# State updates of the decoding streams: a masked stationary operand of 128 rows in place of 32 of its rows

## The chip, the cores and the metric

The kernel runs on one core of a Trainium2 chip. The metric is the device time of one execution in microseconds. TensorE multiplies a stationary operand (up to 128 rows by 128 columns, loaded by an instruction of its own) with a moving operand of the same rows. VectorE, ScalarE and GpSimd work on the 128 partitions of the on-chip memory SBUF, SP issues DMAs.

## The reference

One step of a two-layer streaming encoder: 512 new frames of one prompt, and 16 new frames of each of 8 running streams. Layer 0 is a feed-forward block, then a mixer of four mLSTM heads and sixteen Mamba-2 (SSD) heads, then a feed-forward block; layer 1 has the same with eight gated-DeltaNet heads as its mixer. Each head of each stream carries a state matrix, and the update of these states is what the change touches:

```
C = decay * C + einsum('brh,brhd,brhe->bhde', wr, k, v)                       # mLSTM, 128 x 256 per stream and head
S = exp(bL) * S + einsum('brgj,brgjp,brgn->bgjpn', exp(bL - b) * dt, x, bm)   # SSD, 64 x 128
S = exp(gL) * S + einsum('bhr,bhrd,bhre->bhde', exp(gL - gam), kh, u)         # DeltaNet, 128 x 128
```

The sum over r runs over the 16 frames of one stream. All states of the streams are outputs.

## The kernel before, in words

All 640 frames stand side by side: 512 of the prompt (four tiles of 128) and 8 x 16 = 128 of the streams (tile 4). Matrices of the weights are split into a high and a low part (`split`, ScalarE and GpSimd), and each projection is made of three passes over the parts (`mmT` L225, `projR` L770, `wout` L733; L427 and L494 in the feed-forward blocks). These split operands take one pass of TensorE each; plain fp32 operands, which the recurrences use, take two.

In the mixers the projections are the main line. The recurrences are generators in a list; after six or twelve passes of a projection `tick` advances every generator to its next `yield`. So a step of a recurrence is traced between two packets of projections, and the framework then orders each engine's instructions by the order of tracing and by what is free. `side_by_side` advances a head's prompt and its streams in turn. `until` ticks on without projections where the main line needs a result.

In tile 4 stream b holds the partitions 16 b to 16 b + 15. A row slice starts at a multiple of 32, so one product takes the 32 rows of a pair of streams (g = b // 2), and one of the two operands is zeroed for the other stream of the pair by `par`, a [128, 2] constant with the parity of each partition's stream.

- mLSTM (`mlstm_head`, inner generator `streams`): `kw[:, 4 + e]` holds the weighted keys of tile 4 with parity e alone, made from PSUM at L1289. For each b of 8 one product `kw[32g : 32g + 32, 4 + e]` (stationary) with `v[32g : 32g + 32, 4]` (L1341), then a `yield`, then the update of `Cb[b]` on VectorE (L1343) and its DMA out.
- SSD (`ssd_quad`, inner generator `running(i)`, i = 0, 1): after transposes (L1524) and products of 32 columns (L1531) for each half, two products of 32 rows, `xw[r, 4, ...]` with `Bz[r]` (L1538), where `Bz` holds both parities (L1415).
- DeltaNet (`gdn_streams`, one per head): at the end of a head's chain ScalarE writes `wz`, both parities of w (L2044); then for each g of 4 one product `kw[r, tok]` with `wz[r]` (L2050), two updates on VectorE (L2054) and a DMA per half.

`tmp()` gives one of three rotating SBUF buffers of 128 x 668. A convolution (`conv`, L930 to L963) takes two of them, `gdn_sumsq` one (L1762), `sumsq` and some others one. PSUM in the mixers: two pairs of banks ("big") for projections, four single banks ("small") for the recurrences. ScalarE and VectorE work strictly in order.

Of the kernel before, what the change touches and what calls it, by code (L numbers as in the profile page):

```python
# [11 lines left out]
AF = mybir.ActivationFunctionType  # L12
ALU = mybir.AluOpType
# [3 lines left out]
P = 128  # L17
# [14 lines left out]
class Raw:  # L32


    def __init__(self, load, n=0):
        self.fetch, self.n, self.then, self.v = load, n, None, None
# [17 lines left out]
class Trunk:  # L54
    def __init__(self, ctx, tc, io):
        self.tc, self.nc, self.io = tc, tc.nc, io
        self.cst = ctx.enter_context(tc.tile_pool(name="cst", bufs=1))
        self.sb = ctx.enter_context(tc.tile_pool(name="sb", bufs=1))
        self.dram = ctx.enter_context(tc.tile_pool(name="dram", bufs=2, space=bass.MemoryType.DRAM))
        self.n = 0  # L60
        self.pending = []
        self.bg = []
        self.early = {}
        self.rows = None
        self.ahead = 0
        nc = self.nc

        self.ident = self.const([P, P], "ident")
        make_identity(nc, self.ident)
        self.ones = self.const([P, 1], "ones")  # L70
        nc.vector.memset(self.ones, 1.0)

        self.zero = self.const([P, 1], "zero")
        nc.vector.memset(self.zero, 0.0)


        self.U, self.Ub, self.Bk = (self.const([P, P], n) for n in ("U", "Ub", "Bk"))
        for m in (self.U, self.Bk):
            nc.gpsimd.memset(m, 1.0)
        nc.gpsimd.affine_select(  # L80
            out=self.U, in_=self.U, pattern=[[1, P]], compare_op=ALU.is_ge, fill=0.0, base=0, channel_multiplier=-1
        )
        bk = self.Bk.rearrange("p (b s) -> p b s", s=16)
        nc.gpsimd.affine_select(
            out=bk, in_=bk, pattern=[[-16, 8], [0, 16]], compare_op=ALU.is_ge, fill=0.0, base=0, channel_multiplier=1
        )
        nc.gpsimd.affine_select(
            out=bk, in_=bk, pattern=[[16, 8], [0, 16]], compare_op=ALU.is_ge, fill=0.0, base=15, channel_multiplier=-1
        )
        nc.vector.tensor_tensor(self.Ub, self.U, self.Bk, ALU.mult)  # L90

        self.par = self.const([P, 2], "par")
        st = self.Bk.rearrange("p (g e s) -> p e g s", e=2, s=16)
        for e in range(2):
            nc.vector.tensor_reduce(self.par[:, e : e + 1], st[:, e, :, 0], axis=AX, op=ALU.add)

        self.x = [self.const([P, T], f"x{d}") for d in range(ND)]
        self.xg = [None] * ND
        self.xs = [None] * (ND // 2)
# [1171 lines left out]
    def mlstm_head(self, ab, tile, h, qT, kT, v, sig, qz, nO, nP):  # L1271
        nc, io = self.nc, self.io
        Cb = []
        for b in range(8):
            c = tile("Cb", [P, 257], bufs=8)
# [9 lines left out]
        kw = tile("kw", [P, 6, P], bufs=1)  # L1285
# [39 lines left out]
        def streams():  # L1325
            qs = qT[:, 512:].rearrange("p (g e s) -> p g e s", e=2, s=16)
            qd = qz.rearrange("p (g e) s -> p g e s", e=2)
            for e in range(2):
                nc.scalar.copy(qd[:, :, e, 16 * e : 16 * e + 16], qs[:, :, e])
            yield  # L1330
            inter = self.small()
            for e in range(2):
                for g in range(4):
                    b = 2 * g + e
                    nc.tensor.matmul(inter[32 * g : 32 * g + 32, :257], lhsT=qz[:, b], rhs=Cb[b], start=(e == 0), stop=(e == 1))
            yield
            yield from numerator(4, inter)
            for b in range(8):
                g, e = b // 2, b % 2
                st = self.small()  # L1340
                nc.tensor.matmul(st[:, :257], lhsT=kw[32 * g : 32 * g + 32, 4 + e], rhs=v[32 * g : 32 * g + 32, 4], start=True, stop=True)  # L1341
                yield
                nc.vector.scalar_tensor_tensor(Cb[b], Cb[b], self.dec[:, h, 4 + b : 5 + b], st[:, :257], ALU.mult, ALU.add)  # L1343
                nc.sync.dma_start(out=io["s_C"][b, h], in_=Cb[b][:, :256])
                nc.scalar.copy(nO[:, b * 4 + h : b * 4 + h + 1], Cb[b][:, 256:257])

        yield from self.side_by_side(prompt(), streams())

        den = num[:, :, 256]
# [12 lines left out]
        for e in range(2):  # L1362
# [5 lines left out]
            i = 56 + 2 * h + e  # L1368
# [96 lines left out]
    def ssd_quad(self, tile, u, x, B, Bz, CT, cz, CB):  # L1465

        nc, io = self.nc, self.io
# [16 lines left out]
        xw = tile("xw", [P, NT, 256])  # L1484
# [30 lines left out]

        def running(i):

            inter = self.small()
            j = 2 * u + i
            for hf in range(2):  # L1520
                s0 = S0[2 * i + hf]
                ps = self.small()
                for b in range(4):
                    nc.tensor.transpose(ps[:, b * P : (b + 1) * P], s0[:, b], self.ident)  # L1524
                yield
                S0T = tile("S0T", [P, 4, P], bufs=1)
                nc.scalar.copy(S0T.rearrange("p a b -> p (a b)"), ps)
                for e in range(2):
                    for gg in (2 * hf, 2 * hf + 1):
                        bb = 2 * gg + e  # L1530
                        nc.tensor.matmul(  # L1531
                            inter[32 * gg : 32 * gg + 32, :P], lhsT=cz[:, bb], rhs=S0T[:, bb - 4 * hf], start=(e == 0), stop=(e == 1)
                        )
                yield
                for gg in (2 * hf, 2 * hf + 1):
                    r = slice(32 * gg, 32 * gg + 32)
                    st = self.small()
                    nc.tensor.matmul(  # L1538
                        st[:, :256], lhsT=xw[r, 4, i * P : (i + 1) * P], rhs=Bz[r].rearrange("p a b -> p (a b)"), start=True, stop=True
                    )  # L1540
                    yield
                    for e in range(2):
                        b = 2 * gg + e
                        o = s0[:, b - 4 * hf]
                        nc.vector.scalar_tensor_tensor(o, o, self.dS[:, j, b : b + 1], st[:, e * P : (e + 1) * P], ALU.mult, ALU.add)
                nc.sync.dma_start(out=io["s_ssd"][4 * hf : 4 * hf + 4, 2 * j : 2 * j + 2].rearrange("b h p n -> (h p) b n"), in_=s0)
            y1 = tile("y1", [P, 2, 256])[:, 0, :P].rearrange("p (h d) -> p h d", h=2)
            h = h0 + 2 * i
            nc.vector.tensor_tensor(
                y1,  # L1550
                inter[:, :P].rearrange("p (h d) -> p h d", h=2),
                self.eb[:, 4, h : h + 2].rearrange("p (h o) -> p h o", o=1).to_broadcast([P, 2, 64]),
                ALU.mult,
            )
            o = x[:, 4, i * P : (i + 1) * P]
            nc.vector.tensor_tensor(o, o, y1.rearrange("p h d -> p (h d)"), ALU.add)
# [440 lines left out]
    def gdn_streams(self, tile, h, x, qT, kT, kws, QKs, hl, kqz, square):  # L1997

        nc, io = self.nc, self.io
        t, tok = 4, slice(512, T)  # L2000
# [12 lines left out]
        for g2 in range(2):  # L2013
            ps = self.small()
            for e in range(2):
                for gl in range(2):
                    g = 2 * g2 + gl
# [3 lines left out]
            for gl in range(2):  # L2021
                g = 2 * g2 + gl
# [5 lines left out]
        V, kw, QK = self.Us[h], kws[hl], QKs[hl]  # L2028
        nc.vector.scalar_tensor_tensor(x, kq[:, 0], self.neg[:, h, t : t + 1], x, ALU.mult, ALU.add)
        yield  # L2030
        ps = self.small()
# [5 lines left out]
        ps = self.small()  # L2037
# [4 lines left out]
        wz = kq  # L2042
        for e in (1, 0):
            nc.scalar.activation(out=wz[:, e], in_=w, func=AF.Copy, scale=self.par[:, e : e + 1])  # L2044
        yield
        for g in range(4):
            r = slice(32 * g, 32 * g + 32)
            s0 = S0[g // 2]
            ps = self.small()
            nc.tensor.matmul(ps[:, :256], lhsT=kw[r, tok], rhs=wz[r].rearrange("p a b -> p (a b)"), start=True, stop=True)  # L2050
            for e in range(2):
                b = 2 * g + e
                j = b % 4
                nc.vector.scalar_tensor_tensor(s0[:, j], s0[:, j], self.egs[:, b, h : h + 1], ps[:, e * P : (e + 1) * P], ALU.mult, ALU.add)  # L2054
            if g % 2:
                nc.sync.dma_start(out=io["s_gdn"][4 * (g // 2) : 4 * (g // 2) + 4, h].rearrange("b d e -> d b e"), in_=s0)
            yield

    def gdn_z(self, tile, i):

        zs = tile("zs", [P, NT, 256])
        for t, ps in self.projR(self.w_in, 3072 + 256 * i):
            self.nc.scalar.activation(out=zs[:, t], in_=ps, func=AF.Tanh, scale=self.rch[:, t : t + 1])
            self.nc.vector.scalar_tensor_tensor(zs[:, t], zs[:, t], 1.0, ps, ALU.add, ALU.mult)  # L2064
        self.zs[i] = zs
# [139 lines left out]
```

## Time and profile before

| | |
|---|---|
| median of 3 runs | 2993.99 us (2993.27 to 2996.22) |
| the profiled execution's own time | 2991.16 us |
| its span, first to last instruction | 2989.4 us |
| mean granted TensorE clock | 0.979 of 2.4 GHz |
| TensorE matmuls busy | 2889.4 us |
| TensorE weight loads busy | 2777.9 us |
| VectorE, ScalarE, GpSimd busy | 1877.5, 1250.4, 1478.5 us |

"PE" in the rows is TensorE's matmuls, "PEld" its weight loads, "DVE" VectorE, "ACT" ScalarE, "POOL" GpSimd, "SPq" the queue of SP. A row of the order of time merges neighbouring instructions of one kind: "x2" at a matmul of fp32 operands is one product in two passes. The end of a matmul is modelled, so starts are what to compare.

### The profile page before, as it was taken

The numbers are of one execution on the slowest core, as the hardware profiler recorded it, in microseconds if no ns is written. First come the engines' busy times: TensorE is split into PE (matmuls) and PEld (weight loads), VectorE is DVE, ScalarE is ACT, GpSimd is POOL, SyncE is SP. The second block draws the span as 40 slices with busy tenths as digits, with TensorE's granted clock in tenths as the row PEclk, the third lists the DMA queues.
The fourth block names the chain that finished last, engine by engine and source line by source line (L and its number), as shares of the span: only waits on it lengthen the run. The fifth ranks groups of instructions, "written<-read, shape, count | busy, mean of one in ns | idle before, by whom it ended". The sixth has DMA issues, their size and how long they took to land. (4 is left out here: it accounts for less than half of the span.)

```text
span 2989.4 us, 51425 instructions
## 1 busy us (share of the span) xinstructions
PE 2889.4 (97%) x19910; PEld 2777.9 (93%) x19910; DVE 1877.5 (63%) x3547; ACT 1250.4 (42%) x2655; POOL 1478.5 (49%) x1039
## 2 busy tenths in 40 slices
PE   8999999999999999999999999999999999999997
PEld 7999998988989889999998999999888898999996
DVE  7756655233566677766657666666777756865664
ACT  5333334333344344333344333334555454433334
POOL 3767662222223126776646767633323232677663
PEclk9999999999999999999999999999999999999999
DMA  3322222222213221322221322221221212222212
GB/s 104 106 75 82 76 80 59 87 87 87 84 56 90 73 79 58 102 82 76 81 87 60 99 74 83 75 78 50 64 68 47 85 54 84 71 85 85 85 64 85
DMA packets 243112, 232.14 MB, mean 78 GB/s; under 512 B 22135, under 2 KB 219908, under 8 KB 242870
## 3 DMA queue, kind: packets, MB, share of 16 engines
q1 hardware_dynamic: 242870, 228.87, 25.0%
q8 instruction: 158, 2.59, 0.4%
q14 instruction: 84, 0.69, 0.1%
HBM read 210.23 MB, written 18.60 MB: 77 GB/s over the span
## 5 line engine op out<-in xcount | busy, mean ns | idle before, releaser
L617 POOL TENSOR_TENSOR wsp<-wraw,wsp 128x512 fp32r<-128x512 f32 x600 | 892.2, 1500 | 556.3 <-ACT wsp L616 546.1
L208 POOL TENSOR_TENSOR wsp<-wraw,wsp 128x512 fp32r<-128x512 f32 x216 | 293.4, 1366 | 829.6 <-ACT wsp L207 517.5
L494 PE MATMUL small<-h,wsp 128*128 128x320 f32 x4032 | 597.9, 309 | 0.0
L427 PE MATMUL small<-xg,wsp 128*128 128x320 f32 x3840 | 588.2, 310 | 10.0 <-ACT wsp L616 6.2
L494 PEld LDWEIGHTS small<-h,wsp 128*128 128x128 f32 x4032 | 593.1, 188 | 0.0
L427 PEld LDWEIGHTS small<-xg,wsp 128*128 128x128 f32 x3840 | 570.9, 189 | 12.2 <-ACT wsp L616 7.3
L616 ACT ACTIVATE wsp<-wraw 128x512 fp32r<-128x512 f32 x600 | 364.3, 626 | 373.6 <-PE small L427 216.0
L225 PE MATMUL big<-xg,wsp 128*128 128x320 f32 x2112 | 368.7, 323 | 0.0
L225 PEld LDWEIGHTS big<-xg,wsp 128*128 128x128 f32 x2112 | 321.9, 193 | 21.6 <-issue 20.5
L617 POOL TENSOR_TENSOR wsp<-S,wsp 128x512 fp32r<-128x512 f32 x160 | 250.5, 1577 | 72.0 <-ACT wsp L616 45.0
L427 PE MATMUL small<-extA,wsp 128*128 128x320 f32 x1440 | 254.6, 312 | 1.0 <-POOL wsp L617 1.0
L770 PE MATMUL big<-wsp,xg 128*128 128x256 f32 x1920 | 244.3, 284 | 1.5 <-DVE zs L2064 1.4
L770 PEld LDWEIGHTS big<-wsp,xg 128*128 128x128 f32 x1920 | 233.2, 188 | 4.2 <-DVE zs L2064 2.1
L207 ACT ACTIVATE wsp<-wraw 128x512 fp32r<-128x512 f32 x216 | 136.2, 633 | 224.7 <-PE big L225 99.8
L427 PEld LDWEIGHTS small<-extA,wsp 128*128 128x128 f32 x1440 | 224.2, 190 | 2.5 <-POOL wsp L617 2.3
L454 DVE TENSOR_TENSOR up<-small,up 128x320 f32<-128x320 f32 x200 | 97.5, 488 | 201.3 <-PE small L427 201.2
L454 DVE TENSOR_TENSOR gate<-small,gate 128x320 f32<-128x320 f32 x200 | 97.9, 490 | 143.9 <-PE small L427 142.5
L427 PE MATMUL small<-extB,wsp 128*128 128x320 f32 x960 | 180.9, 310 | 0.0
L579 DVE SCALAR_TENSOR_TENSOR x<-small,x 128x320 f32<-128x320 f32 x368 | 157.9, 480 | 29.9 <-PE small L494 29.1
L485 ACT ACTIVATE h<-up 128x1280 fp32r<-128x1280 f32 x40 | 51.0, 1274 | 263.8 <-DVE up L483 263.8
L427 PEld LDWEIGHTS small<-extB,wsp 128*128 128x128 f32 x960 | 152.0, 189 | 0.0
L616 ACT ACTIVATE wsp<-S 128x512 fp32r<-128x512 f32 x160 | 99.3, 627 | 112.2 <-PE small L427 59.6
(469 smaller groups left out, 4057.6 us busy)
## 6 DMA issues: line engine op xcount, KB each, us to landing
wraw<-in_ffn_w_up SPq DMA_DIRECT2D x43, 1024.0 KB
wraw<-in_ffn_w_gate SPq DMA_DIRECT2D x43, 1024.0 KB
wraw<-in_ffn_w_down SPq DMA_DIRECT2D x38, 1024.0 KB
wraw<-in_ab_w_in SPq DMA_DIRECT2D x16, 1024.0 KB
wraw<-in_gdn_w_in SPq DMA_DIRECT2D x16, 1024.0 KB
wraw<-in_ffn_w_down SPq DMA_DIRECT2D x16, 512.0 KB
wraw<-in_ab_w_out SPq DMA_DIRECT2D x32, 256.0 KB
wraw<-in_ab_w_in SPq DMA_DIRECT2D x12, 512.0 KB
```

The lines of the kernel that those rows point to most:

```text
L207: nc.scalar.activation(out=hi, in_=src[:, i : i + n], func=AF.Copy)
L208: nc.gpsimd.tensor_tensor(lo, src[:, i : i + n], hi.bitcast(F32), ALU.subtract)
L225: self.nc.tensor.matmul(ps[:, half, :HT], lhsT=wp, rhs=ap[:, half * HT : half * HT + HT], start=(k == 0 and i == 0), stop=(k == n - 1 and ...
L427: self.nc.tensor.matmul(ps, lhsT=unit.parts[wp][:, k], rhs=acts[k][:, ap], start=(first and k == 0 and i == 0), stop=(last and k == ND // ...
L454: nc.vector.tensor_tensor(c(dst), bank[b], c(src), ALU.add)
L485: nc.scalar.activation(out=hi, in_=u, func=AF.Copy)
L494: self.nc.tensor.matmul(out[half], lhsT=wp, rhs=ap[:, half * HT : half * HT + HT], start=(first and i == 0), stop=(last and i == 2))
L579: nc.vector.scalar_tensor_tensor(x[:, i], out[i], 0.5, x[:, i], ALU.mult, ALU.add)
L616: nc.scalar.activation(out=u.parts[0], in_=src, func=AF.Copy)
L617: nc.gpsimd.tensor_tensor(u.parts[1], src, u.parts[0].bitcast(F32), ALU.subtract)
L770: self.nc.tensor.matmul(ps[:, t % 2, :256], lhsT=ap[:, t * P : (t + 1) * P], rhs=wp, start=(k == 0 and i == 0), stop=(k == ND - 1 and i == 2))
```

## The change

Two constants are added beside `par`: `one` [128, 8], whose column b is one at the partitions of stream b and zero elsewhere, and `duo` [128, 4], the same for the pairs of streams. A stationary operand is then copied by ScalarE with such a column as its scale per partition, so that the rows of the other streams are zero, and the product runs over all 128 rows.

- mLSTM: before streams 0 and 4 of a head, four copies (one per stream) into a "tmp" buffer, then a `yield`; the products use all rows of `kb` and `v`.
- SSD: a new helper `per_duo` makes four copies (one per pair) into a "tmp" buffer at the start of `running(i)`.
- DeltaNet: `per_duo` of the keys after `wz`, then a `yield`.

Four 128 x 128 copies make one group; there are 8 groups per mixer kind. The number of products, their outputs, updates and DMAs stay.

```diff
+        self.one = self.const([P, 8], "one")
+        nc.vector.tensor_copy(self.one, bk[:, :, 0])
+        self.duo = self.const([P, 4], "duo")
+        od = self.one.rearrange("p (g e) -> p g e", e=2)
+        nc.vector.tensor_tensor(self.duo, od[:, :, 0], od[:, :, 1], ALU.add)
...
             for b in range(8):
                 g, e = b // 2, b % 2
+                if b % 4 == 0:
+                    kb = self.tmp()[:, :512].rearrange("p (b c) -> p b c", b=4)
+                    for i in range(4):
+                        nc.scalar.activation(out=kb[:, i], in_=kw[:, 4 + i % 2], func=AF.Copy, scale=self.one[:, b + i : b + i + 1])
+                    yield
                 st = self.small()
-                nc.tensor.matmul(st[:, :257], lhsT=kw[32 * g : 32 * g + 32, 4 + e], rhs=v[32 * g : 32 * g + 32, 4], start=True, stop=True)
+                nc.tensor.matmul(st[:, :257], lhsT=kb[:, b % 4], rhs=v[:, 4], start=True, stop=True)
                 yield
...
         def running(i):
 
+            xg = self.per_duo(xw[:, 4, i * P : (i + 1) * P])
             inter = self.small()
...
-                    r = slice(32 * gg, 32 * gg + 32)
                     st = self.small()
                     nc.tensor.matmul(
-                        st[:, :256], lhsT=xw[r, 4, i * P : (i + 1) * P], rhs=Bz[r].rearrange("p a b -> p (a b)"), start=True, stop=True
+                        st[:, :256], lhsT=xg[:, gg], rhs=Bz.rearrange("p a b -> p (a b)"), start=True, stop=True
                     )
...
+        kg = self.per_duo(kw[:, tok])
+        yield
         for g in range(4):
-            r = slice(32 * g, 32 * g + 32)
             s0 = S0[g // 2]
             ps = self.small()
-            nc.tensor.matmul(ps[:, :256], lhsT=kw[r, tok], rhs=wz[r].rearrange("p a b -> p (a b)"), start=True, stop=True)
+            nc.tensor.matmul(ps[:, :256], lhsT=kg[:, g], rhs=wz.rearrange("p a b -> p (a b)"), start=True, stop=True)
...
+    def per_duo(self, src):
+
+        out = self.tmp()[:, :512].rearrange("p (g c) -> p g c", g=4)
+        for g in range(4):
+            self.nc.scalar.activation(out=out[:, g], in_=src, func=AF.Copy, scale=self.duo[:, g : g + 1])
+        return out
```

## Rows read from the trace of the kernel before

**Rows 1.** The page: busy time, share of the span and instructions of each engine.

```profile
PE 2889.4 (97%) x19910; PEld 2777.9 (93%) x19910; DVE 1877.5 (63%) x3547; ACT 1250.4 (42%) x2655; POOL 1478.5 (49%) x1039
```

**Rows 2.** Busy time by stretch: PE, PEld, DVE, ACT, POOL, then clock, DMA.

```profile
545.00:770.00 225.00, 217.48 (x1476) 192.31 (x1476) 79.33 (x204) 81.17 (x242) 54.81 (x43) 0.98 0.28 84
842.00:1060.00 218.00, 214.06 (x1485) 186.42 (x1484) 143.23 (x328) 91.57 (x240) 50.15 (x36) 1.00 0.26 75
2140.00:2470.00 330.00, 320.20 (x2383) 290.06 (x2382) 226.73 (x669) 172.70 (x530) 87.18 (x75) 0.94 0.23 64
```

**Rows 3.** TensorE in order of time, first mLSTM head: start us, us, line, form.

```profile
550.23 0.59 PE L1311 MATMUL small<-extC,extB 128*128 128x257 f32 x2
550.66 0.60 PE L1313 MATMUL small<-v,kw 128*128 128x257 f32 x2
551.18 0.70 PE L1341 MATMUL small<-v,kw 32*128 32x257 f32 x2
```

**Rows 4.** The weight loads there; in brackets the idle time before them.

```profile
550.45 0.41 PEld L1313 LDWEIGHTS small<-v,kw 128*128 128x128 f32 x2
551.18 0.29 PEld L1341 LDWEIGHTS small<-v,kw 32*128 32x128 f32 x2 [0.33 <-issue]
551.81 0.44 PEld L225 LDWEIGHTS big<-xg,wsp 128*128 128x128 f32 x3 [0.33 <-issue]
```

**Rows 5.** TensorE in order of time: packets around 560, 1055 and 2234 us.

```profile
559.75 0.69 PE L1341 MATMUL small<-v,kw 32*128 32x257 f32 x2
...
561.46 0.70 PE L1341 MATMUL small<-v,kw 32*128 32x257 f32 x2
...
1054.16 0.69 PE L1538 MATMUL small<-Bz,xw 32*128 32x256 f32 x2
...
1055.87 0.69 PE L1538 MATMUL small<-Bz,xw 32*128 32x256 f32 x2
...
2233.21 0.69 PE L2050 MATMUL small<-kq,kw 32*128 32x256 f32 x2
...
2234.91 0.69 PE L2050 MATMUL small<-kq,kw 32*128 32x256 f32 x2
```

**Rows 6.** The page's groups: projection passes of the feed-forward blocks, busy us, mean ns.

```profile
L494 PE MATMUL small<-h,wsp 128*128 128x320 f32 x4032 | 597.9, 309 | 0.0
```

**Rows 7.** The three lines with 32 rows: passes, ns min/median/max, first and last start.

```profile
L1341 PE MATMUL small<-v,kw x64: 375/427/480, 548.6 to 765.7; 32*128 32x257 f32 x64
...
L1538 PE MATMUL small<-Bz,xw x64: 374/426/478, 842.7 to 1056.2; 32*128 32x256 f32 x64
...
L2050 PE MATMUL small<-kq,kw x64: 374/478/791, 2141.4 to 2460.7; 32*128 32x256 f32 x64
```

**Rows 8.** ScalarE's copy with a parity column as scale: ns min/median/max.

```profile
L2044 ACT ACTIVATE kq<-kq,par x16: 384/398/404, 2140.6 to 2453.3; 128x128 f32<-128x128 f32 x16
```

**Rows 9.** What TensorE waited for, 2140 to 2470: us, times, longest.

```profile
PE small L1785 <- DVE kap L1779: 2.1, 1, 2.1
...
PE small L2050 <- ACT kq L2044: 0.7, 2, 0.6
```

**Rows 10.** VectorE in order of time: a convolution and the next one's first step.

```profile
774.89 0.49 DVE L937 TENSOR_TENSOR tmp<-big,R 128x320 f32<-128x320 f32 x1 [1.02 <-PE big L225]
...
780.55 1.02 DVE L959 SCALAR_TENSOR_TENSOR extA<-tmp,tmp 128x512 f32<-128x512 f32 x2 [0.89 <-ACT tmp L956]
781.93 0.49 DVE L937 TENSOR_TENSOR tmp<-big,R 128x320 f32<-128x320 f32 x1 [0.36 <-PE big L225]
```

**Rows 11.** Weight loads by line, 545 to 770: busy, mean ns, idle before.

```profile
L1341 PEld LDWEIGHTS small<-v,kw 32*128 32x128 f32 x64 | 9.4, 183 | 9.0 <-issue 5.7 <-ACT extA L1303 1.3 <-DVE nr L357 1.2
...
L1311 PEld LDWEIGHTS small<-extC,extB 128*128 128x128 f32 x24 | 4.0, 188 | 0.0
```

**Rows 12.** Busy time in two stretches of the pairs (columns as in rows 2).

```profile
2254.60:2264.80 10.20, 10.20 (x35) 8.34 (x34) 7.05 (x18) 2.73 (x6) 0.50 (x2) 0.50 0.66 186
2336.50:2350.10 13.60, 13.60 (x51) 11.40 (x52) 6.64 (x19) 2.03 (x6) 1.52 (x2) 0.50 0.77 233
```

## The prediction

> **What bounds the kernel now.** I read the shares of the five engines first: TensorE is busy for 97% of the span, VectorE for 63%, ScalarE for 42% [rows 1]. Then the same shares in the three stretches that the change touches (545 to 770 us: mLSTM heads; 842 to 1060: SSD quads; 2140 to 2470: DeltaNet pairs): TensorE 217 of 225, 214 of 218 and 320 of 330 us, and no other engine over 70% [rows 2]. So in each of them the projections of the main line keep TensorE fed, and the recurrences run in the gaps between packets of six projection matmuls. A busy TensorE is not one at its peak, though, and the same rows show it: its weight loads are busy for only 192 of 225, 186 of 218 and 290 of 330 us, where elsewhere they follow the matmuls closely. Some time inside those stretches is counted as busy in which nothing new is loaded.
>
> The order of time on TensorE shows where. An fp32 product is two passes, each with its load. Two neighbouring products of 128 rows and 257 columns start 0.43 us apart [rows 3], so a pass is 0.215 us. The product of 32 rows behind them starts 0.52 us after its predecessor [rows 3], and the load of the next projection 0.63 us after that. On the load side the 128-row loads run on without a hole, while the first 32-row load stands 0.33 us idle, and so does the first projection load after it [rows 4]. The profile names no engine that the load waits for ("issue"). I read this as TensorE letting the matmuls in flight end before the rows in use change from 128 to 32, and again on the way back.
>
> **The price of one such product.** I take a clean packet: six projection passes and one 32-row product, nothing else. It repeats every 1.71 us in an mLSTM head, every 1.71 in an SSD quad, every 1.70 in a DeltaNet pair [rows 5]. A projection pass of 320 columns is 597.9 / 4032 = 0.148 us by the largest group of such passes [rows 6]; six are 0.89. A 128-row product is 0.43. 1.71 - 0.89 - 0.43 = 0.39 us is lost per product, whatever the stage. (It shows as about 0.09 ahead, 0.2 within, 0.1 behind.)
>
> **The change part by part.**
>
> *Removed: the 32-row products.* Each of the three lines has 64 passes, which is 32 products [rows 7]; 96 in all. Each stands alone among 128-row work, so each pays its switch in and out. With 128 rows the operands differ from the neighbours' in nothing but values. The sum: 96 x 0.39 = -37.4 us, on TensorE, in stretches where TensorE sets the pace. The matmul count stays at 96 x 2 passes; rows that the mask zeroes cost nothing extra if a 128-row pass costs its 0.215 us, as the neighbours' do. The bounds: nothing (if a masked product keeps the cost) and -37.4. I take -37.4, since the row nearest to the new product, with the same 128 x 257 shape [rows 3], is a measured one.
>
> *A rule that speaks against it.* The 128-row load of L1313 begins at 550.45 while the matmuls of L1311, of the same rows, run until 550.82 [rows 3, 4]. The Trainium skill, "TensorE: Matmul & The Clock Gate", section "Part 3: Packing small matmuls — row/col tiling", says that a weight load overlaps matmuls in flight only where its row group differs. By that rule a full-height load would stand bare on every pass, and the change would gain nothing; by the row the load is hidden and the sum is -37.4. The trace disagrees with the rule here, and I go by the trace.
>
> *Added: 96 masking copies on ScalarE.* 24 groups of four 128 x 128 copies with a scale per row: 8 in the heads (before stream 0 and stream 4), 8 in the quads (one per half quad), 8 in the pairs (one per head). The same operation, SBUF to SBUF with a mask column as scale, takes 0.40 us in L2044 [rows 8]: 1.6 us per group, 38 us in all. ScalarE is busy for 81 of 225, 92 of 218 and 173 of 330 us [rows 2], so the work fits. What hides it: in heads and pairs the generator yields after the copies, so a packet of projections (0.89 us) and whatever else is due stands ahead of the first product, which needs the first copy alone; in the quads two yields, four transposes and four 32-column products come first. Queued behind the copies on ScalarE are the splits of the next weights and the copies out of PSUM; both run ahead of TensorE by some packets. If the cover is gone, a group costs up to 1.6 us, 24 x 1.6 = 38 us. Where it is thin already is seen: twice TensorE waits for the masking copy L2044 right before L2050, 0.7 us together [rows 9]. There the four new copies come right after L2044; I take +2 us, between 0 and 38, near the row.
>
> *Added: two yields per head of the mLSTM, one per head of the DeltaNet.* Each moves the remaining steps of a stream, with their output DMAs and the loads that SP has queued behind them, one packet later (1.3 to 1.7 us). The main line makes its next demand on these heads many packets later, so I take 0; a bare step would cost its packet.
>
> *Added: the waits.* The products now wait for ScalarE's copy; behind one on TensorE's queue stand the next projections. ScalarE waits for a free "tmp" buffer; this is a rival below. In the forecast it costs nothing: a convolution holds its two of three buffers from 774.89 to 781.57 us, and the next starts its multiplications at 781.93, when both are free again [rows 10]. A third one held by the masked copies is one that the convolutions can do without, by 0.36 us.
>
> *Added: two small VectorE operations at the start* (a copy of 8 columns, a sum of 4). They stand behind a mask product that waits for the same GpSimd operation, long before their first use: 0.
>
> *Late next.* Where TensorE comes sooner to a product that waits for VectorE's chains, part of what is saved turns into waiting. The largest such wait in the pairs is 2.1 us, in one place [rows 9]. I take +1 us.
>
> **The sum.** -37.4 + 2 + 1 = -34.4 us on the profiled execution of 2991.16 us (span 2989.4, 1.8 around it): 2956.8. The median of the three runs lies 2.8 us above that execution, so 2959.6 for a median; I say 2959.
>
> **Rivals.**
>
> 1. *Nothing comes of it:* a full-height product in this place loses as much as a 32-row one, since each of its two loads (188 ns for the loads of L1311 [rows 11]) stands bare. 2 x 0.19 = 0.38 against 0.39 saved: about 2993. Against: the same rows show idle time ahead of the loads of L1341 (9.0 us over 64) and none ahead of those of L1311. Chance 0.05. (The rule of the Trainium skill that is weighed above would make this case; the overlap in the trace is why it gets no more.)
>
> 2. *The copies stand in front of the products* in half of the groups, because ScalarE is in order and a weight split of 0.6 us or a convolution step of 0.9 gets in between: 12 x 1.6 = 19 us given back, 2959 + 17 = 2976. For it: the two waits for L2044. Against: ScalarE's idle share. Chance 0.14.
>
> 3. *Slower, by the "tmp" buffers.* The copies of quads and pairs (16 groups) hold one of the three over the four products, some 7 us or more. If a convolution then has to wait for its second buffer, or the copies for a convolution's (up to the 6.7 us from 774.89 to 781.57), ScalarE or VectorE stands, the two PSUM pairs of the projections stay full, and TensorE stops. It decides at 37.4 / 16 = 2.3 us per group; at half a convolution, 3.35 us, it is +54 - 37 = +17: 3011. For it: the DeltaNet's squares take a "tmp" as well. Against: the 0.36 us above, and two PSUM pairs that let TensorE go on. Chance 0.07.
>
> 4. *More than the sum, by the clock.* Two stretches around the products of the pairs, 10.2 and 13.6 us, ran at a granted clock of 0.50, the lower level of 1.2 GHz [rows 12]; ahead of both TensorE had short waits, and thin work. Without the holes they may stay at 2.4 GHz: half of 23.8 us is 11.9, so 2947. Against: other thin work stays. Chance 0.10.
>
> The forecast itself has 0.64.
>
> **How the numbers follow.** What a measurement here can tell from no change is about 0.2%, 6 us. Faster: forecast, rivals 2 and 4, 0.88. Same: rival 1, 0.05. Slower: rival 3, 0.07. The range goes from 2949, which takes in part of rival 4, to 2975, which takes in the milder half of rival 2; left out are some 0.2: rivals 1 and 3 (0.12), and the outer parts of 2 and 4.
>
> **What would show it.** In the changed profile the clean packet of six projections and one product should repeat every 1.32 us in place of 1.71, in all three stages; the two passes of a product should last 0.59 to 0.60 us together, like those of L1311 and L1313 [rows 3], in place of 0.69 to 0.70 [rows 5]; the idle time ahead of its loads and ahead of the projections behind it should be gone. TensorE's waits for the new copies should stay under 4 us in all. Wrong would be: packets that stay at 1.7 us (rival 1), a wait of TensorE for the copies in the first rows of its waits (rival 2), waits for "tmp" ahead of convolutions or copies and TensorE idle behind them (rival 3), other stretches of the lower clock (rival 4).

## The result, and the profile after

The changed kernel takes 2947.25 us (median of 4 runs, 2944.59 to 2951.37); the kernel before took 2995.1 in the same sitting (4 runs). The ratio is 0.9847, with an interval from 0.9834 to 0.9859. The forecast was 2959: right in sign, 12 us too slow, and 2 us below the lower end of its range (2949). The profiled execution went from 2991.16 to 2948.21 us, which is -42.95 where the prediction's sum on that execution was -34.4.

The first line of the page of the profile, to be set against [rows 1]: TensorE's matmuls are busy for 50 us less, its loads for 5.5 us less, and ScalarE for 24 us more.

```profile
PE 2839.5 (96%) x19910; PEld 2772.4 (94%) x19910; DVE 1894.1 (64%) x3549; ACT 1274.1 (43%) x2751; POOL 1477.3 (50%) x1039
```

TensorE in order of time after the change, to be set against [rows 3, 5] (start us, us, line, form):

```profile
550.04 0.59 PE L1317 MATMUL small<-extC,extB 128*128 128x257 f32 x2
550.47 0.60 PE L1319 MATMUL small<-v,kw 128*128 128x257 f32 x2
550.90 0.59 PE L1352 MATMUL small<-v,tmp 128*128 128x257 f32 x2
551.15 1.25 PE L231 MATMUL big<-xg,wsp 128*128 128x320 f32 x6
...
558.80 0.59 PE L1352 MATMUL small<-v,tmp 128*128 128x257 f32 x2
...
560.11 0.60 PE L1352 MATMUL small<-v,tmp 128*128 128x257 f32 x2
...
1030.14 0.59 PE L1549 MATMUL small<-Bz,tmp 128*128 128x256 f32 x2
...
1031.46 0.59 PE L1549 MATMUL small<-Bz,tmp 128*128 128x256 f32 x2
...
2209.24 0.60 PE L2062 MATMUL small<-kq,tmp 128*128 128x256 f32 x2
...
2210.56 0.59 PE L2062 MATMUL small<-kq,tmp 128*128 128x256 f32 x2
```

The state product now stands in line like any other: it starts 0.43 us after L1319, as L1319 does after L1317, and the projection follows 0.25 later (0.63 before). The clean packet repeats every 1.31, 1.32 and 1.32 us in the three stages, where it was 1.71, 1.71 and 1.70. On the load side there, no idle time is left (it would stand in brackets at the end of a line), against 0.33 us twice in [rows 4]:

```profile
550.25 0.41 PEld L1319 LDWEIGHTS small<-v,kw 128*128 128x128 f32 x2
550.69 0.40 PEld L1352 LDWEIGHTS small<-v,tmp 128*128 128x128 f32 x2
551.12 1.01 PEld L231 LDWEIGHTS big<-xg,wsp 128*128 128x128 f32 x6
```

The three lines again, answering to [rows 7] (passes, ns min/median/max, first and last start):

```profile
L1352 PE MATMUL small<-v,tmp x64: 377/380/382, 550.9 to 753.8; 128*128 128x257 f32 x64
...
L1549 PE MATMUL small<-Bz,tmp x64: 377/378/484, 835.1 to 1037.2; 128*128 128x256 f32 x64
...
L2062 PE MATMUL small<-kq,tmp x64: 377/380/484, 2123.5 to 2418.3; 128*128 128x256 f32 x64
```

From first to last start, the heads' products shrink from 217.1 to 202.9 us, the quads' from 213.5 to 202.1, the pairs' from 319.3 to 294.8. The first two are -14.2 and -11.4, against -12.5 foreseen for each (32 x 0.39); the third is -24.5, twice what was foreseen. Why, the clock shows. Below are the mixer stages whole, first of the kernel before, then after (bounds from the first product of a mixer's input projections to the first down projection behind it; columns as in [rows 2]):

```profile
465.80:1109.40 643.60, 622.66 (x4312) 561.08 (x4313) 333.71 (x770) 256.34 (x679) 165.93 (x121) 0.99 0.26 78
...
1996.80:2521.00 524.20, 497.95 (x3679) 459.37 (x3679) 355.51 (x994) 269.84 (x766) 151.53 (x129) 0.94 0.22 63
```

```profile
467.30:1090.30 623.00, 599.33 (x4313) 570.13 (x4313) 335.07 (x770) 272.24 (x744) 163.96 (x121) 0.98 0.27 81
...
1977.10:2477.10 500.00, 473.77 (x3678) 447.08 (x3679) 357.11 (x993) 276.73 (x796) 152.51 (x129) 0.97 0.23 66
...
2122.00:2427.40 305.40, 294.70 (x2381) 277.18 (x2381) 227.62 (x675) 178.08 (x555) 88.05 (x74) 0.99 0.24 69
...
2172.00:2178.80 6.80, 6.66 (x28) 5.55 (x29) 2.43 (x8) 4.16 (x13) 1.72 (x2) 0.50 0.13 42
```

The DeltaNet stage went from 524.2 to 500.0 us while its clock rose from 0.94 to 0.97. Half clock is 1.2 in place of 2.4 GHz; among the pairs' products one stretch of it is left, 6.8 us long. [rows 12] show two, of 10.2 and 13.6 us, but the clock records of the trace of before hold six between 2140 and 2470 us, 41 us in all. Half of the 34 us that went is 17 of the -24.5, which leaves some 7 for the products. So the profile after already says that two things happened. The feed-forward stages did not move (887.4 and 886.8 us for the middle one).

### The profile page after: what moved, and what is told of

The parts are those of the page before. It is cut to its first block, busy times and chain, and to the rows that moved or that the text cites. A ratio compares the mean times of both kernels' runs of the same rounds, so it can differ in the third digit from the quotient of the medians.

```text
span 2946.5 us, 51522 instructions
## 1 busy us (share of the span) xinstructions
PE 2839.5 (96%) x19910; PEld 2772.4 (94%) x19910; DVE 1894.1 (64%) x3549; ACT 1274.1 (43%) x2751; POOL 1477.3 (50%) x1039
## 5 line engine op out<-in xcount | busy, mean ns | idle before, releaser
L214 POOL TENSOR_TENSOR wsp<-wraw,wsp 128x512 fp32r<-128x512 f32 x216 | 292.8, 1363 | 787.5 <-ACT wsp L213 390.9
```

What stands on the lines that cost most here:

```text
L214: nc.gpsimd.tensor_tensor(lo, src[:, i : i + n], hi.bitcast(F32), ALU.subtract)
```

## How the runs are told apart

Every run lists its mean granted clock, and for this kernel that number carries most of the scatter: 46 runs of the kernel before, in three sittings, lie between 2978.0 and 2998.3 us at clocks of 0.984 down to 0.976, but time x clock stays within 2926 to 2934 us (mean 2930.1). I call time x clock the *work* of a run, and the rest, time x (1 - clock), its *clock loss*. This is exact only where TensorE sets the pace, and the clock's last digit is worth 3 us in one run, so means over a kernel's runs are used. Where the text gives the time at half clock in a stage, it is that of one execution, the profiled one.

| kernel | median us (range) | ratio to before [interval] | work | clock loss |
|---|---|---|---|---|
| before | 2994.6, 2993.2, 2985.8 by sitting | 1 | 2930.1 | 60 |
| after | 2947.25 (2944.6 to 2951.4) | 0.9847 [0.9834, 0.9859] | 2901.9 | 45.7 |
| e1_rows32 | 2981.75 (2978.7 to 2984.0) | 0.9964 [0.9948, 0.9981] | 2931.5 | 50.3 |
| e4_rows64 | 2979.19 (2974.7 to 2981.3) | 0.9952 [0.9936, 0.9968] | 2930.5 | 48.3 |
| e2_gdn_only | 2967.36 (2965.7 to 2970.6) | 0.9915 [0.9892, 0.9938] | 2923.2 | 44.5 |
| e3_ab_only | 2964.77 (2961.3 to 2968.9) | 0.9907 [0.9885, 0.9928] | 2910.1 | 54.9 |
| e5_together | 2976.1 (2967.5 to 2977.8) | 0.9947 [0.9928, 0.9966] | 2915.7 | 58.6 |
| e7_no_copies | 2945.92 (2944.4 to 2948.0) | 0.9859 [0.9833, 0.9886] | 2901.9 | 44.2 |
| e8_yield_only | 2975.18 (2972.5 to 2979.6) | 0.9950 [0.9937, 0.9963] | 2929.6 | 45.5 |
| e9_no_yields | 2950.8 (2948.0 to 2958.3) | 0.9880 [0.9854, 0.9907] | 2901.8 | 50.2 |
| e10_no_mlstm_yields | 2939.53 (2936.8 to 2948.9) | 0.9857 [0.9831, 0.9882] | 2899.3 | 41.9 |
| e11_yield_early | 2979.29 (2971.7 to 2984.8) | 0.9974 [0.9959, 0.9990] | 2926.0 | 52.7 |
| e12_wide_sums | 2981.57 (2976.3 to 2989.5) | 0.9986 [0.9970, 1.0001] | 2934.6 | 47.1 |
| e13_best | 2955.68 (2950.3 to 2960.9) | 0.9903 [0.9883, 0.9924] | 2907.6 | 48.0 |

e1 to e4 shared one sitting, e5 to e9 a second, e10 to e13 a third.

## The experiments

**e1_rows32: everything of the change but the rows in use.** Copies, yields, masks and the order on every engine are those of the changed kernel.

```diff
-nc.tensor.matmul(st[:, :257], lhsT=kb[:, b % 4], rhs=v[:, 4], ...)
+nc.tensor.matmul(st[:, :257], lhsT=kb[32 * g : 32 * g + 32, b % 4], rhs=v[32 * g : 32 * g + 32, 4], ...)
```
(likewise in the quads and the pairs)

> The changed kernel with every instruction in the same place and order on every engine; only the 96 products read 32 rows of the masked operands (the rows of their pair) in place of 128. Theory 1 (the loss sits in the change of the rows in use): each product loses 0.39 us again, 37 us in all, and the stretches at the lower clock in the DeltaNet pairs come back with the holes (some 10 us): about 2995. Theory 2 (the loss per product comes back, but the clock gain of the pairs comes from the new order of the work, which stays): about 2985. Theory 3 (a good part of the gain is the new order, not the rows): 2960 to 2975.

2981.75 us, near theory 2: the rows alone are worth 34.5 us (to 2947.25, of another sitting), and all the rest of the change 13 against its sitting's 2994.6. By work, the rows give 2931.5 - 2901.9 = 29.6 us and the rest nothing (+1.4), so the 13 are clock. The order of time shows the old gap come back with the old rows, 0.63 us from product to projection:

```profile
555.24 0.70 PE L1352 MATMUL small<-v,tmp 32*128 32x257 f32 x2
555.87 1.15 PE L231 MATMUL big<-xg,wsp 128*128 128x320 f32 x6
```

**e4_rows64: the same with 64 rows** (`kb[64 * (g // 2) : ...]` and so on).

> As the run before, the same order on every engine, but the products read 64 rows (the half that holds their pair) of the masked operands. Theory 1 (any change of the rows in use costs, whatever their number): as with 32 rows, about 2985 to 2995, packets of six projections and one product 1.71 us apart. Rival (the cost grows with the rows left unused): between, about 2960 to 2970, packets 1.5 us apart.

2979.19 us, work 2930.5: 64 rows cost what 32 do (theory 1). What is paid for is that a product uses fewer rows than its neighbours, not how few:

```profile
556.66 0.70 PE L1352 MATMUL small<-v,tmp 64*128 64x257 f32 x2
557.29 1.00 PE L231 MATMUL big<-xg,wsp 128*128 128x320 f32 x5
```

**e2_gdn_only and e3_ab_only: the change in the DeltaNet alone, and in the mLSTM and SSD heads alone.**

> The change in the DeltaNet pairs alone (32 of the 96 products). By the comparison of the traces the DeltaNet stage became 24 us shorter, of which 12.5 are 32 products and the rest the clock: 2971. If the gain of the clock there is chance or comes from what lies ahead of the stage: 2982.

> The change in the mLSTM heads and SSD quads alone (64 of the 96 products). 64 x 0.39 = 25 us, less the new wait of 4 us at 782 us and the lower clock behind it: 2974. If the stages are independent of each other the gains of this run and the run before add up to that of the whole change, 48 us.

By time they give 27 and 30 us, together more than the whole, and more than the 24 and 21 expected. By work they add up: -6.9 and -20.0, sum -26.9, against -28.2 for the whole. The overlap is in the clock: e2 has a loss of 44.5, e3 of 54.9, the whole of 45.7. The change in the pairs is worth 6.9 us of work, not 12.5; the one in heads and quads 20.0, where 25 less a stop of 4 was expected.

**e7_no_copies: unmasked operands of 128 rows.**

```diff
-nc.tensor.matmul(st[:, :257], lhsT=kb[:, b % 4], rhs=v[:, 4], ...)
+nc.tensor.matmul(st[:, :257], lhsT=kw[:, 4 + e], rhs=v[:, 4], ...)
```
(no copies in any of the three places, so the sums run over the rows of other streams too and the states are not those of the reference)

> The changed kernel without the 96 masking copies: the products read all 128 rows of the unmasked operands (so the states sum over all streams: that part of the computation is changed), the yields stay. Theory (the copies are hidden beside the projections): 2945 to 2950, as the changed kernel. Rival (half of the groups stand in front of TensorE): some 19 us faster, 2928.

2945.92 us, work 2901.9, as with the copies. 96 copies are free here, although ScalarE works on them for 33 us. Groups of the changed kernel by line and form, with the idle time before them in the last column:

```profile
L1349 ACT ACTIVATE tmp<-kw,one 128x128 f32<-128x128 f32 x32 | 11.5, 419 | 0.0
...
L2075 ACT ACTIVATE tmp<-kw,duo 128x128 f32<-128x128 f32 x32 | 10.9, 394 | 0.1
...
L2075 ACT ACTIVATE tmp<-xw,duo 128x128 f32<-128x128 f32 x32 | 10.9, 418 | 0.9 <-DVE xw L1496 0.9
```

**e8_yield_only: the kernel before, with one line more in the DeltaNet, ahead of the four products; 32 rows, no copies.**

```diff
         yield
+        yield
         for g in range(4):
             r = slice(32 * g, 32 * g + 32)
```

> The kernel before with one thing of the change: a second yield before the four products in the DeltaNet heads, no masks, no copies, 32 rows. Theory (the 13 us between the kernel before and the run with 32 rows of the masked operands is the clock, and the clock comes from where the steps of the pairs fall): granted clock 0.983 and about 2982 in nearly every run. Rival (the copies or what they do to ScalarE's order are needed for it): 0.979 and 2995.

2975.18 us, 7 less than the theory had: a bare `yield` is worth 15 us by the ratio (18 by the medians). Its work is that of the kernel before (2929.6 against 2930.1); all of it is clock loss, 45.5 in place of 61.0 in that sitting. The DeltaNet stage by itself, to be set against the row of before above (524.20 us at 0.94):

```profile
1997.90:2504.20 506.30, 483.37 (x3679) 446.11 (x3679) 357.94 (x994) 268.34 (x766) 153.30 (x129) 0.97 0.23 65
```

The trace's clock records hold 58 us at half clock in that stage before, 26 here, 27 after the change.

**e9_no_yields: the changed kernel without its added yields** (two per mLSTM head, one per DeltaNet head).

> The changed kernel without its added yields (one before each group of four in mLSTM, one in each DeltaNet head): the first product of a group comes right behind its copies. If TensorE then stands for the first copy in 16 groups, up to 16 x 0.4 = 6 us, or 16 x 1.6 = 26 us where it waits for all four: 2953 to 2973. If the order of the instructions covers it: 2947.

2950.8 us, work 2901.8, loss 50.2 (44 to 59 over its four runs) against 61.0 in its sitting. So the yields are not needed for the work, and the DeltaNet's yield is not the only thing that shifts the pairs: with it gone the copies and the shorter products still leave 27 us at half clock in the DeltaNet stage, where before has 58. Which of the two does it, no run shows.

**e10_no_mlstm_yields: only the mLSTM's yields out.** In the changed kernel TensorE's loads stand for 4.14 us at 782.7, ahead of L739.

> The changed kernel without the added yield ahead of streams 0 and 4 of an mLSTM head; the yield ahead of the DeltaNet's products stays. Theory A (the 4.1 us that TensorE stands at L739 at 782.5 us and the 6.8 us of half clock behind it come from that yield, which puts the tanh of a convolution ahead of a weight split): the stop and the stretch are gone, 4.1 + 3.4 = 7.5 us less, 2940. Theory B (such stops move with any order of steps and come back at another place): within 3 us of the changed kernel, 2944 to 2950.

The stop is gone. TensorE's waits at L739 between 466 and 835 us, first of the changed kernel, then of this one:

```profile
PE big L739 <- DVE tmp L945: 3.9, 1, 3.9
```

```profile
PE big L739 <- DVE x L752: 0.3, 1, 0.3
```

The same wait of 3.8 or 3.9 us stands in all kernels that have these yields (after, e1, e3, e4, e7, e13) and in none of the others; so the yields bring it. My reason for it, a tanh ahead of a weight split, was wrong: TensorE waits for a PSUM pair that the next convolution reads, and VectorE is late with three convolutions in a row. The changed kernel's last one in order of time (start, duration; by line, the three steps of L958 there last 958, 1828 and 911 ns):

```profile
779.24 3.77 DVE L958 SCALAR_TENSOR_TENSOR tmp<-tmp,taps,tmp 128x664 f32<-128x664 f32 x3 [1.06 <-ACT tmp L952]
...
780.04 1.32 POOL L214 TENSOR_TENSOR wsp<-wraw,wsp 128x512 fp32r<-128x512 f32 x1 [0.54 <-ACT wsp L213]
...
783.89 1.98 DVE L965 SCALAR_TENSOR_TENSOR extA<-tmp,tmp 128x512 f32<-128x512 f32 x2 [0.88 <-ACT tmp L962]
```

And the same steps without those yields:

```profile
779.96 2.80 DVE L958 SCALAR_TENSOR_TENSOR tmp<-tmp,taps,tmp 128x664 f32<-128x664 f32 x3 [1.06 <-ACT tmp L952]
...
781.92 1.99 POOL L214 TENSOR_TENSOR wsp<-wraw,wsp 128x512 fp32r<-128x512 f32 x1 [1.97 <-ACT wsp L213]
...
783.65 1.02 DVE L965 SCALAR_TENSOR_TENSOR extA<-tmp,tmp 128x512 f32<-128x512 f32 x2 [0.89 <-ACT tmp L962]
```

Where a step of L958 starts soon behind GpSimd's L214 (here 0.20 us, in the two convolutions before 0.57 and 0.14), the step takes 1.83 us or a little more in place of 0.91. Where L214 starts just behind a step, it is L214 that takes 1.99 in place of 1.32, and VectorE runs on. The whole trace of the changed kernel bears it out: the 94 steps of L958 that start while GpSimd has no such operation under way take 0.86 to 0.91 us each; of the 14 that start beside one, ten take 1.26 to 1.93. The convolutions repeat every 7.5 to 8.5 us in the one kernel and every 7.0 in the other. The Trainium skill has such a contention: "GPSIMD Engine Reference", "1. Specifications", says that GpSimd shares its SBUF interfaces with VectorE and that VectorE's instructions with two SBUF inputs contend for them; L958 has two. Which engine comes second is a matter of the order of steps. That this is what makes VectorE late for the pair of banks is read from the two traces; no run changes it alone.

What the stop is worth is less sure: the work falls by 2.6 us, and 2939.53 is the lowest median of all, but in its sitting the kernel before ran at 2985.8 too. The ratios, 0.9857 and 0.9847, don't part the two kernels.

**e11_yield_early: the kernel before, with the added yield ahead of L2032 instead.**

> The kernel before with one yield added in the DeltaNet's streams ahead of the product of L2032 and none at the products of the states; all rows as before. Theory A (any shift of the DeltaNet's steps by a packet takes the stretches of half clock away): granted clock 0.983 or more, half-clock time in the pairs below 30 us instead of 58, 2975 to 2982. Theory B (the yield must stand right ahead of the four products, where it separates them from the thin sums before): clock 0.979 to 0.980, 2990 to 2996.

2979.29 us, loss 52.7 against 57.7 in its sitting; the DeltaNet stage had 34 us at half clock. The time agrees with theory A, its bound of 30 us for the half clock is missed, its clock of 0.983 is reached in four of ten runs, and the ratio (0.9974) gives only 8 us, 3 of them work, where e8 had 15 (0.9950). A shift elsewhere helps too, but less.

**e12_wide_sums: the one-column sums of squares made 64 columns wide; order as before.**

```diff
-self.nc.tensor.matmul(ps[:, t : t + 1], lhsT=sq[:, t * P : (t + 1) * P], rhs=self.ones, ...)
+self.nc.tensor.matmul(ps[:, 64 * t : 64 * t + 64], lhsT=sq[:, t * P : (t + 1) * P], rhs=self.ones.to_broadcast([P, 64]), ...)
```

> The kernel before with the DeltaNet's sums of squares (L1765) written as products of 64 equal columns in place of one; the order of steps as before, all values used are the same. Theory A (the clock falls where these one-column products stand between waits of TensorE): half-clock time in the pairs falls from 58 us to under 30, 2978 to 2984. Theory B (it falls where TensorE waits, whatever the columns of the products beside): 50 to 60 us stay, 2990 to 2997.

**e13_best: the same edit on the changed kernel.**

> The changed kernel with the sums of squares of 64 equal columns in place of one; a candidate to beat both. Theory A of the run with wide sums alone: the 27 us of half clock that are left in the pairs fall below 12, 2940. Theory B: the same as the changed kernel, 2944 to 2950.

e12 seems to say yes (24 us at half clock in the stage, time 2981.57 as theory A had it), but its ratio, 0.9986, can't be told from 1, because its work grew by 4.5 us: the wide products are not free. And e13 says no: the same edit leaves 31 us at half clock where the changed kernel has 27 (its profile is of the run with the lowest clock, 0.981), its loss over four runs is 48.0 against 45.7, and the kernel is slower than either theory had it (2955.68, work 2907.6 against 2901.9). So that the narrow products bring the low clock is not shown; e12 fits a mere shift of the steps as well.

**e5_together: the kernel before, with its 32-row products back to back,** four (two in the quads) into as many PSUM banks, the updates behind them.

> From the kernel before, without masks: products of 32 rows, but the four of a group (two in an SSD half) follow each other with no packet of projections between them, each in its own PSUM bank, and the updates come after the next yield. Theory (the loss belongs to the change of the rows in use, in and out, and not to the product): 32 groups x 0.39 = 12.5 us lost in place of 37.4, so 25 us faster than before, about 2970 at the clock of before; if in addition four products on four different sets of rows run beside each other, up to 27 us more, about 2943. Rival (each product has its price): 2995. Second rival (four of the four single PSUM banks at once make the recurrences wait): slower than 2995.

2976.1 us, work 2915.7, loss 58.6; the theory had 2970. If the price is paid at the change of rows, a bunch should pay it once, and its length agrees. Four products and the way back to the projections take 1.28 us, where four single ones took 4 x (0.43 + 0.39) = 3.3:

```profile
548.73 1.35 PE L1341 MATMUL small<-v,kw 32*128 32x257 f32 x8
550.01 1.14 PE L225 MATMUL big<-xg,wsp 128*128 128x320 f32 x6
...
548.73 0.30 PEld L1341 LDWEIGHTS small<-v,kw 32*128 32x128 f32 x6 [0.33 <-issue]
549.39 0.29 PEld L1341 LDWEIGHTS small<-v,kw 32*128 32x128 f32 x2 [0.35 <-DVE num L1301]
```

1.28 is also less than four times 0.43, so products on different rows run partly side by side: six loads, those of three products, take 0.30 us together. But the work falls by 14.4 us alone, against 25 expected and 28.2 for the change. The four banks are all that the recurrences have, and TensorE now waits for other things in the DeltaNet stage (4.3 us in all for the DMA of `S`, 3.5 for L1766, where before has 0 and 0.5). That would be 7 of the 11 us that are missing; that the banks are the reason is not shown.

## Why the prediction was right and wrong

*The mechanism and its price were right.* 0.39 us per product was read off the packets, and the packets changed by 0.38 to 0.40. In the mLSTM and SSD stage e1 takes 652.2 us with 30.7 at half clock, the changed kernel 623.0 with 20.5; half of each half-clock time taken off, 636.9 against 612.7: 24.2 us for 64 products, 25.0 foreseen. "Nothing comes of it" (rival 1) is out. The two mixer stages of e1, to be set against those of the changed kernel above:

```profile
466.00:1118.20 652.20, 628.42 (x4313) 566.52 (x4313) 337.17 (x770) 274.10 (x744) 163.11 (x121) 0.98 0.26 77
2005.00:2511.40 506.40, 483.83 (x3679) 446.94 (x3679) 358.29 (x994) 278.00 (x798) 152.39 (x129) 0.97 0.23 65
```

Where in a packet the 0.39 us lie, the starts of the single passes in the trace of before tell: 0.09 ahead of the product's first pass, 0.10 between its two passes (0.32 from start to start, 0.22 with 128 rows), 0.09 ahead of the first projection and 0.10 behind that one (0.25, else 0.15). Whether the 0.10 inside the product comes from the change of rows, as the prediction has it, or from any pass that follows another on the same 32 rows, no run shows: in e5 the fourth product of a bunch has its passes 0.32 apart as well.

TensorE's loads of the same rows stay hidden: 64 loads of L1352 of 187 to 193 ns add nothing to the packets. The rule in the Trainium skill, "TensorE: Matmul & The Clock Gate", "Part 3: Packing small matmuls — row/col tiling", by which they would stand bare, fails here as it did in the trace of before; the same section also says that a load for the background weight buffer is pulled ahead of matmuls in flight, which would fit. The Trainium skill, "TensorEngine Tiling (Array Packing)", "Key Properties", says that a change of the tiling mode drains TensorE; the 0.33 us of idle loads at 32 rows and e4 at 64 agree with it.

*The pairs' term of -37.4 was mis-sized.* There e1 takes 506.4 us with 27.3 at half clock, the changed kernel 500.0 with as much: 6.4 us for 32 products, where 12.5 were foreseen. In the pairs TensorE is not the only one that is late. Waits that the changed kernel has between 2120 and 2430 us and e1, with the same order, has not:

```profile
PE small L1971 <- DVE nr L362: 1.8, 1, 1.8
...
PE small L905 <- DVE nr L362: 0.8, 1, 0.8
PE small L2029 <- DMA S<-in_state_gdn: 0.7, 1, 0.7
...
PE small L873 <- DVE nr L363: 0.4, 1, 0.4
...
PE small L2062 <- DVE S L2001: 0.3, 1, 0.3
PE small L1971 <- DVE o L1983: 0.3, 1, 0.3
```

These are 4.3 of the 6.1 us that are missing; the prediction had +1 for them, in one place. The rest I have not placed.

*"+2" for the copies was too much.* No wait of TensorE for L1349 or L2075 is in the trace, and e7 gains nothing in work by leaving them out. Rivals 2 and 3 did not happen: neither copies nor buffers stop anything.

*"I take 0" for the added yields failed, twice.* The mLSTM's yields brought the stop at 782.7 us, 4.1 us long (2.6 us of work by e10). The DeltaNet's yield, put into the kernel before by itself, brings 15 us of clock (e8). In the changed kernel it is not what most of that hangs on: without any added yield the loss is still 50.2, against 61.0 before and 45.7 with them (e9). The prediction asked what the yields delay and found it to be due late, which was true; it did not ask what an order one packet later does to two engines that contend, and to the clock.

*The clock was put down as a rival when it was a term beside the others.* In the profiled executions the loss went from 62.8 to 47.2 us: -15.6 of the -42.95, where the forecast had 0. The size was close to rival 4's 11.9, which took two of the six stretches for its price. Its reason, the holes, does not hold as it stands: e1 and e8 keep all 32-row products and their holes, and have no more half clock in the DeltaNet stage (27 and 26 us) than the changed kernel (27). So the holes by themselves do not hold the clock down, and another order of steps in the pairs is enough to bring it up; which detail of the order decides is open. Whether taking out the holes would have been enough in the old order is open too, since no run does that without the copies. Of all the kernels here the one before has the largest loss, 60 us; the others lie 1 to 18 below it, e3 and e5 (5 and 1) within the scatter of their runs.

So the forecast's -34.4 was -27.3 in work (-34.4 foreseen: 6 less in the pairs, some 3 to 4 lost at 782.7, against 2 for the copies and 1 for waits that the sum held already) and -15.6 in clock. The two errors ran against each other, so that the number came as near as it did is in part luck; and a range that takes in "part of rival 4" but not all of the forecast and the clock together ended 2 us too early.

## What to carry to other kernels

A lone product that uses fewer rows of TensorE than its neighbours costs more than one of 128 rows (0.39 us here), and idle time of the weight loads that the profile puts down to no engine ("issue") shows it. Widening it with zeros is cheap where another engine has room for the mask; bunching such products saves part of it, if there is room for their results. Price such an edit by the repeat of a clean packet, stage by stage, and expect all of it only where TensorE alone is late. And before reading a gain of one per cent as the edit's, multiply each run's time by its granted clock: one empty step more per DeltaNet head moved this kernel by 15 us.

## What the runs showed of the hardware that was not expected

- 64 rows cost as much as 32 (e4: 0.63 us from a product to the projection behind it, as in e1; 0.25 with 128).
- A step of VectorE with two SBUF inputs takes 1.83 us in place of 0.91 when it starts 0.1 to 0.6 us behind GpSimd's split (the changed kernel); the other way round the split takes 1.99 in place of 1.32 (e10).
- Four fp32 products of 32 different rows each, back to back, take 1.28 us with the change back, less than four products of 128 rows one after the other (4 x 0.43 = 1.72; e5).
- One kernel, unchanged, ran at granted clocks from 0.976 to 0.984 and so from 2998 to 2978 us, with its work within 0.3% throughout; in the second sitting twelve of its sixteen runs stood at 0.976 to 0.980 (2992 to 2998 us), four at 0.982 and 0.983 (2982 to 2985), and none between.
